# Row sums of the modulation, one per step and tied to VectorE's latest scan operation, in a GLA and SSD backbone

## The chip, the cores and the metric

The kernel runs on one NeuronCore of a Trainium2 chip. The metric is the device time of one execution in microseconds (us). The engines are TensorE (PE, matmuls), VectorE (DVE), ScalarE (ACT), GpSimd (POOL) and SyncE (SP, which issues the DMAs). Each engine works its instructions off in the order in which the program lists them, and waits for the others through semaphores.

## What is computed

A two-layer backbone over 512 latent and 256 context tokens of width 1024. Layer 0 mixes tokens by bidirectional gated linear attention (GLA, 4 heads), layer 1 by a Mamba-2 scan (SSD); each is followed by a squared-ReLU MLP, and each sub-layer is modulated by six vectors, for latent and context tokens apart.

```python
for i in range(DEPTH):
    ...
    m_l = jnp.split((s_lat @ ada_w[i] + ada_b[i])[:, None, :], 6, axis=-1)
    m_c = jnp.split(s_ctx @ ada_w[i] + ada_b[i], 6, axis=-1)
    ul = snake(modulate(hl, m_l[0], m_l[1]))
    uc = modulate(hc, m_c[0], m_c[1])
    ...
    hl = layer_norm(DEEPNORM_ALPHA * hl + m_l[2] * snake(yl), ln_g[i, 0], ln_b[i, 0])
    hl = layer_norm(DEEPNORM_ALPHA * hl + m_l[5] * sq_relu_mlp(modulate(hl, m_l[3], m_l[4]), ffn_w1[i], ffn_w2[i]),
                    ln_g[i, 1], ln_b[i, 1])
    ...
```

Here DEPTH is 2, `hl` and `hc` are the latent and the context tokens, and `yc, yl` come from the mixer of the layer, given `uc, ul`.

Inside one head of the GLA mixer, with q, k of width 128 and v of width 256:

```python
cum = jnp.cumsum(gi, axis=2)
diff = cum[:, :, :, None, :] - cum[:, :, None, :, :]
decay = jnp.exp(jnp.where(mask, diff, -jnp.inf))
attn = jnp.einsum('bhid,bhjd,bhijd->bhij', qi, ki, decay)
o = jnp.einsum('bhij,bhjv->bhiv', attn, vi) + jnp.einsum('bhid,bhdv->bhiv', qi * jnp.exp(cum), s)
```

`gi` is the log decay of a chunk and `s` the state that the chunks before it left.

## The kernel before

Activations lie transposed, features on the 128 partitions and the 768 tokens along the free axis. A product of float32 accuracy is made of three matmuls over split operands: ScalarE rounds a weight tile to its high half (`wh`, L218), VectorE subtracts to get the low half (`wl`, L219), and PE runs high by high, low by high and high by low (L265; L547 for the values). `worked(cols)` counts the columns of these matmuls; every 768 make one unit, and the units are the clock by which other work is woven in while the program is written out.

Two lists hang on that clock. `side` holds generators that say after each step how many units to wait for the next. `background` holds the row sums: one step every `pace[0]` units.

**Row sums.** `ada_rows` computes those modulation vectors that aren't made by matmuls. For each item (layer, m) and block b of 128 rows it loads a 128x1024 weight block (`rawa`, SP, three buffers, which the thrown-away output `junk` shares in the GLA layer) and runs one scalar_tensor_tensor with a row sum (L172) for each of the two streams; for layer 1's later vectors only the latent stream is needed. A step covers one block, so two row sums for most blocks. `behind()` lists a row sum directly behind the instruction held in `evacv`, if one is held. Before the change `evacv` is set only in the two functions that take FFN and output products out of PSUM, so in the whole GLA scan part it is empty, and the scheduler of the program places the row sums freely.

**GLA.** `head(h)` makes q, k, v and two gate projections for one head on PE. The scan of the head before it, `scan(h-1)`, runs as a `side` generator at the same time, so scans 1 to 3 lie beside the projections of heads 1 to 3 and scan 4 beside the output projection. A scan starts from the log decays W (L590), and then goes through seven levels, s = 1, 2, ..., 64. In a level ScalarE takes exponentials of W into E (L629, L630), VectorE multiplies them by q and k (L631), GpSimd and VectorE update W (L639 to L642), PE makes the score blocks from E (L601), and VectorE copies the scores of the level before into A under a mask (L620; L617 for s = 64). Then W becomes the decayed q and k (the decay products, L653 and L654, in two halves), PE transposes them (L664), makes the state updates (L672), VectorE chains the states (L683, L685), PE makes outputs (L703), which are normalized (L705 to L708), transposed (L730) and gated (L731). This last part, from the decay products on, is called the tail.

**FFN.** `ffn` runs its two products in blocks of eight row tiles, with its own paces for the row sums of layer 1, which run beside it.

Of the kernel before, what the change touches and what calls it, by code (L numbers as in the profile page):

```python
# [13 lines left out]
ALU = mybir.AluOpType  # L14
PSUM = bass.MemoryType.PSUM

P = 128
# [43 lines left out]
def tile_backbone(ctx, tc, xT, cc, cr, vecs, rows, ada_w0, ada_wr, lnf, ffn_w1, ffn_w2,  # L61
# [52 lines left out]
    evacv = [None]  # L114

    def behind():
        return tc.issue_after(evacv[0].ins) if evacv[0] else nullcontext()
# [30 lines left out]
    def ada_rows(items, alloc, junk):  # L148
        srow = [alloc(s) for s in range(2)]
        for s in range(2):  # L150
            nc.sync.dma_start(srow[s], cr[s:s + 1, :].to_broadcast([P, D]))
            nc.scalar.activation(srow[s], srow[s], AF.Silu)
        def load(layer, m, b):
            raw = wpool.tile([P, D], F32, tag="rawa", name=nm("rawa"), bufs=3)
            nc.sync.dma_start(raw, ada_wr[48 * layer + 8 * m - 16 + b])
            return raw

        todo = [(layer, m, b) for layer, m in items for b in range(8)]
        raws = [load(*todo.pop(0))]
        yield  # L160
        for layer, m in items:
            streams = range(1 if layer and m > 1 else 2)
            t = ct([P, 8, 2], f"row{layer}{m}")
            nc.gpsimd.memset(t, 0.0)
            for b in range(8):
                if todo:
                    raws.append(load(*todo.pop(0)))
                raw = raws.pop(0)
                for s in streams:
                    o = raw if s == streams[-1] else junk()  # L170
                    with behind():
                        nc.vector.scalar_tensor_tensor(o, raw, 1.0, srow[s], ALU.mult, ALU.mult, accum_out=t[:, b, s:s + 1])  # L172
                yield
            c0 = V_ADA + 48 * layer + 8 * m
            nc.vector.tensor_tensor(t, t, vec[:, c0:c0 + 8].unsqueeze(2).to_broadcast([P, 8, 2]), ALU.add)
            mods[layer, m] = t
# [211 lines left out]
    def ffn(layer, xs, acc, segs, pool, npre, presegs, restsegs, passes, after):  # L388
# [27 lines left out]
        for bi, nb in enumerate((8, 8, 8, 8 - nlast, nlast)):  # L416
            ms = range(h0, h0 + nb)
            if bi == 0:
# [6 lines left out]
                for m in ms[:npre]:  # L425
                    f1(m, restsegs, held[m])
                pace[0] = 19
                ms = ms[npre:]
# [6 lines left out]
            if bi == 0:  # L435
                gate = mod(layer, 5)
                pace[0] = 22
            if bi < 4:
# [48 lines left out]
    def gla_layer(xs, first):  # L487
# [20 lines left out]
        background.append(ada_rows([(0, 2), (0, 3), (0, 4)], lambda s: xn_tile(f"srow{s}"), lambda: wpool.tile([P, D], F32, tag="rawa", name=nm("junk"), bufs=3)))  # L508
        pace[0] = 12
        aT = gp.tile([P, NT], F32R, tag="aT", name="aT")  # L510
# [41 lines left out]
        def head(h):  # L552
# [19 lines left out]
            if h == 0:  # L572
                pace[0] = 22
            side.append(scan(h, qk, v, gs, yt))

        def scan(h, qk, v, gs, yt):
# [38 lines left out]
            def level(s, E):  # L615
                if s == HP:
                    scores(E[:, 1, :], E[:, 0, :], lambda b, a, sp, bs, qs: (nc.scalar.copy, nc.vector.tensor_copy)[b](a, sp), 1)  # L617
                else:
                    scores(qk[:, 1, :] if s == 1 else E[:, 1, :], E[:, 0, :],
                           lambda b, a, sp, bs, qs: nc.vector.copy_predicated(  # L620
                               a, lvm[s][bs, qs].unsqueeze(1).to_broadcast(half), sp))

            for s in (1, 2, 4, 8, 16, 32, 64):
# [6 lines left out]
                nc.scalar.activation(Ev[:, 0:na, :, 0, :], Wv[:, 2:2 + na, :, 0, :], AF.Exp, scale=1.0 / 16)  # L630
                nc.vector.tensor_mul(E[:, 0:na, :], E[:, 0:na, :], qk[:, 0:na, :])  # L631
                bc = [P, nb, s]
# [8 lines left out]
                nc.vector.tensor_add(Wv[:, 0, :, 1, :], Wv[:, 0, :, 1, :], Wv[:, 0, :, 0, s - 1:s].to_broadcast(bc))  # L641
                nc.vector.tensor_add(Wv[:, 2, :, 0, :], Wv[:, 2, :, 0, :], Wv[:, 2, :, 1, 0:1].to_broadcast(bc))  # L642
                yield LV[h][0]
# [8 lines left out]
            for a, b in ((1, 1), (0, 0)):  # L652
                nc.scalar.activation(W[:, a:4:2, :], W[:, a:4:2, :], AF.Exp, scale=1.0 / 16)  # L653
                nc.vector.tensor_mul(W[:, a:4:2, :], W[:, a:4:2, :], qk[:, b:b + 1, :].to_broadcast([P, 2, NT]))  # L654
            yield 1
# [24 lines left out]
            def step(S, i, a, d):  # L680
                t = new_S()
                if S is None:
                    nc.vector.tensor_copy(t, d[:, 1 - a, :])  # L683
                else:
                    nc.vector.scalar_tensor_tensor(t, S, dec[:, a, i:i + 1], d[:, 1 - a, :], ALU.mult, ALU.add)  # L685
                return t
# [8 lines left out]
            def output(c):  # L695
# [9 lines left out]
                nc.scalar.activation(on[:, c, :], op, AF.Square, accum_out=rs)  # L705
                nc.vector.tensor_scalar(rs, rs, 1.0 / 256, RMS_EPS, ALU.mult, ALU.add)
                nc.gpsimd.tensor_tensor(rs, rs, mhalf[:, 0:1], ALU.pow)
# [17 lines left out]
            for c2 in range(2):  # L725
                for c0, c1 in SEG:
                    pt = sm_ps([P, 4, P])
                    ts = slice(c0 * P, c1 * P)
                    for c in range(c0, c1):
                        nc.tensor.transpose(pt[:, c - c0, :], on[:, c, c2 * P:(c2 + 1) * P], ident)  # L730
                    nc.vector.scalar_tensor_tensor(yt[c2][:, ts], pt.rearrange("p c t -> p (c t)")[:, :(c1 - c0) * P],  # L731
                                                   vec[:, V_GN + c2:V_GN + c2 + 1], gs[c2][:, ts], ALU.mult, ALU.mult)
# [519 lines left out]
    with phase("fp") as fp:  # L1252
        pace[0] = 21
        background.append(ada_rows([(0, 5)] + [(1, m) for m in range(6)],
# [93 lines left out]
```

## Time and profile before

| what | value |
| --- | --- |
| median of 3 runs | 1938.48 us (1937.09 to 1941.59) |
| profiled execution, its own time | 1938.47 us |
| its span | 1936.8 us |
| instructions in the span | 28836 |
| row sums (L172), 128x1024, those that write over their input, x80 | 99.7 us, mean 1252 ns |
| weight split, low half (L219) x225 | 271.1 us, mean 1208 ns |
| score matmuls and projections of scans 1 to 3 | about 95 to 310 us of the span |
| first FFN, PE without a gap | 447 to 957 us |

The page of a profile gives busy time by engine, the chain of work that ended last (followed back from the last instruction to what released each step), and groups of instructions by line. In a timeline row stand the start, the duration in us, the engine, the line, the operation with output and inputs, the count, and in brackets the idle time ahead of it with what ended it. In a row of stretches stand the stretch, its length, the busy time of the engines or of the chosen instructions, TensorE's granted clock as a share of full speed, the DMA share and GB/s.

### The profile page before, as it was taken

Reading aid. Unit: us, or ns where it says so; the run is one execution under the profiler, and the core shown is the slowest. Engines: PE = TensorE matmul, PEld = TensorE weight load, DVE = VectorE, ACT = ScalarE, POOL = GpSimd, SP = SyncE. Lnnn points to the kernel's source line nnn. Section 1 sums busy time; section 2 is a strip of 40 time slices with the busy share of each in tenths; the row PEclk is TensorE's granted clock in tenths of the full one; section 3 lists DMA queues with packets and bytes.
Section 4 is the critical chain, followed back from the end, with each engine's and each line's share of the span. In section 5 each row is a group of like instructions: output and inputs, shape, how many; then the busy total and the mean of one; then the engine's idle time right before and its main releaser. Section 6 shows DMA issues by size and latency. Waiting matters only on the chain.

```text
span 1936.8 us, 28836 instructions
## 1 busy us (share of the span) xinstructions
PE 1877.8 (97%) x11365; PEld 1602.2 (83%) x11365; DVE 1265.8 (65%) x1932; ACT 795.8 (41%) x1387; POOL 392.4 (20%) x363
## 2 busy tenths in 40 slices
PE   7989999999999999999998999999999999999997
PEld 5978898788888888888897778888877788888886
DVE  4998877977655434433477989999896673333345
ACT  4445456456213113112274555556564452323231
POOL 2033241302102002000001333323331321102012
PEclk9999999999999999999999999999999999999999
DMA  9624203122444444323225333343443523333331
GB/s 354 192 73 134 77 26 98 38 91 89 151 134 123 135 129 133 120 93 98 66 68 136 120 115 121 113 126 127 131 125 115 170 71 97 98 98 98 95 90 54
DMA packets 78999, 219.07 MB, mean 113 GB/s; under 512 B 11088, under 2 KB 15824, under 8 KB 78864
## 3 DMA queue, kind: packets, MB, share of 16 engines
q1 hardware_dynamic: 78864, 217.24, 35.7%
q8 instruction: 89, 1.46, 0.3%
q14 instruction: 46, 0.38, 0.1%
HBM read 209.07 MB, written 8.13 MB: 112 GB/s over the span
## 4 chain that ended last, share of the span: by engine, by line
PE 60%; DVE 17%; issue 9%; ACT 6%; POOL 4%; DMA 4%; SPq 1%; DVEq 0%; ACTq 0%; POOLq 0%
PE mm L265 53%; DVE cv L911 4%; DMA L<-crowc 2%; DVE cf L914 2%; DVE wl L219 1%; DVE A L620 1%; PE sm L703 1%; POOL L L1048 1%; POOL W L639 1%; PE mm L547 1%; DVE E L631 1%; DMA raw<-in_ada_w_dram 1%; POOL ssum L1089 1%; DVE lnst L330 1%; ACT xn L340 1%
## 5 line engine op out<-in xcount | busy, mean ns | idle before, releaser
L265 PE MATMUL mm<-xh,wh 128*128 128x512 f32 (+1 forms) x1800 | 551.3, 360 | 2.2 <-ACT xh L1096 2.2
L265 PE MATMUL mm<-xl,wh 128*128 128x512 f32 (+1 forms) x1800 | 545.3, 356 | 3.8 <-DVE xl L1097 3.8
L265 PE MATMUL mm<-xh,wl 128*128 128x512 f32 (+1 forms) x1800 | 543.5, 355 | 0.8 <-DVE wl L219 0.8
L218 ACT CAST wh<-raw 128x1024 fp32r<-128x1024 f32 (+3 forms) x225 | 226.1, 1006 | 656.9 <-PE mm L265 621.1
L219 DVE TENSOR_TENSOR wl<-raw,wh 128x1024 fp32r<-128x1024 f32 (+3 forms) x225 | 271.1, 1208 | 199.5 <-ACT wh L218 195.7
L265 PEld LDWEIGHTS mm<-xl,wh 128*128 128x128 f32 x1800 | 300.8, 189 | 55.4 <-DVE xl L1097 5.0
L265 PEld LDWEIGHTS mm<-xh,wh 128*128 128x128 f32 x1800 | 300.1, 189 | 53.8 <-issue 4.7
L265 PEld LDWEIGHTS mm<-xh,wl 128*128 128x128 f32 x1800 | 298.8, 189 | 50.1 <-issue 2.0
L410 POOL TENSOR_TENSOR rq<-rr 128x768 f32<-128x768 f32 (+1 forms) x62 | 102.4, 1652 | 735.5 <-ACT rr L409 732.7
L446 DVE SCALAR_TENSOR_TENSOR acc<-mm,row,acc 128x256 f32<-128x256 f32 (+1 forms) x182 | 100.6, 580 | 212.6 <-PE mm L265 212.2
L265 PE MATMUL mm<-rh,wh 128*128 128x512 f32 x704 | 215.1, 359 | 0.0
L265 PE MATMUL mm<-rl,wh 128*128 128x512 f32 x704 | 212.5, 355 | 0.0
L265 PE MATMUL mm<-rh,wl 128*128 128x512 f32 x704 | 212.4, 355 | 0.0
L911 DVE SCALAR_TENSOR_TENSOR cv<-pre,cvec,cv 128x770 f32<-128x770 f32 (+1 forms) x128 | 149.7, 1170 | 12.6 <-ACT cv L909 10.8
L265 PEld LDWEIGHTS mm<-rl,wh 128*128 128x128 f32 x704 | 117.0, 189 | 21.4
L265 PEld LDWEIGHTS mm<-rh,wl 128*128 128x128 f32 x704 | 115.3, 188 | 20.3
L265 PEld LDWEIGHTS mm<-rh,wh 128*128 128x128 f32 x704 | 116.1, 188 | 19.2
L412 DVE TENSOR_TENSOR rl<-rq,rh 128x768 fp32r<-128x768 f32 (+2 forms) x67 | 53.3, 795 | 76.2 <-POOL rq L410 75.9
L172 DVE SCALAR_TENSOR_TENSOR rawa<-rawa,srow 128x1024 f32<-128x1024 f32 x80 | 99.7, 1252 | 0.8
L1045 ACT ACTIVATE L<-L,lcol 128x128 f32<-128x128 f32 x256 | 80.1, 393 | 0.0
L1048 POOL TENSOR_TENSOR L<-L,L 128x512 f32<-128x512 f32 x32 | 49.0, 1530 | 151.1 <-ACT L L1045 151.1
L958 POOL TENSOR_SCALAR_AFFINE_SELECT L<-L 128x512 f32<-128x512 f32 x64 | 53.6, 838 | 119.5 <-DMA L<-crowc 111.1
(295 smaller groups left out, 2514.2 us busy)
## 6 DMA issues: line engine op xcount, KB each, us to landing
raw<-in_ffn_w_dram SPq DMA_DIRECT2D x112, 512.0 KB, 3.8
rawa<-in_ada_wr_dram SPq DMA_DIRECT2D x80, 512.0 KB, 3.6
raw<-in_ssd_w_in_dram SPq DMA_DIRECT2D x48, 512.0 KB, 3.6
L<-crowc SPq DMA_DIRECT2D x64, 256.0 KB, 3.8
raw<-in_ada_w_dram SPq DMA_DIRECT2D x16, 512.0 KB, 9.2
raw<-in_gla_w_in_dram SPq DMA_DIRECT2D x16, 512.0 KB, 4.5
ec<-crow SPq DMA_DIRECT2D x64, 128.0 KB, 2.9
acc<-in_xT_dram SPq DMA_DIRECT2D x14, 384.0 KB, 6.9
```

Source lines behind the costliest of these rows:

```text
L172: nc.vector.scalar_tensor_tensor(o, raw, 1.0, srow[s], ALU.mult, ALU.mult, accum_out=t[:, b, s:s + 1])
L218: nc.scalar.copy(h, src)
L219: nc.vector.tensor_sub(l, src, h.bitcast(F32))
L265: nc.tensor.matmul(part_of(ps, t0, n), a[:, k, :], b[:, t0:t0 + n], start=(k == 0 and i == 0), stop=(k == kt - 1 and i == 2))
L410: eng.tensor_mul(q[:, a:b], r[:, a:b], r[:, a:b])
L412: evacv[0] = nc.vector.tensor_sub(rl[:, a:b], q[:, a:b], rh[:, a:b].bitcast(F32))
L446: evacv[0] = nc.vector.scalar_tensor_tensor(acc[m][:, t0:t0 + n], part_of(ps, t0, n), gate[:, m, s:s + 1], (src or acc)[m][:, t0:t0 + n], ...
L911: nc.vector.scalar_tensor_tensor(c[:, 0:n], pre[:, t:t + n], cw(t), c[:, 0:n], ALU.mult, ALU.add)
L914: nc.vector.scalar_tensor_tensor(f[:, t0:t1], f[:, t0:t1], 1.0, c[:, t0 + d:t1 + d], ALU.add, ALU.mult)
L958: nc.gpsimd.affine_select(out=L[z], in_=L[z], compare_op=ALU.is_ge, fill=NEG, base=0, pattern=[[0, 4], [1 - 2 * z, P]], channel_multiplier ...
L1045: nc.scalar.activation(t[:, h, :], t[:, h, :], AF.Exp, bias=lcol[:, c, r:r + 1])
L1048: nc.gpsimd.tensor_add(L[0], L[0], L[1])
```

## The change

Four things change. `ada_rows` gives out one row sum per step, not a block's pair. The paces are about halved (12 to 6 and 22 to 11 in the GLA layer, 19 to 10, 22 to 12 and 21 to 11 around the first FFN), so that about as many row sums come per unit where blocks have two, and twice as many where blocks have one. A helper `mark` puts an instruction into `evacv`, and seven places in the scan use it: the masked score copies, the multiply of E, the second update of W, the decay products, the state steps, the variance of the outputs and the gated outputs. So from the first scan on a row sum is listed behind the latest of these.

```diff
+    def mark(ins):
+        evacv[0] = ins
+
@@ ada_rows
                     with behind():
                         nc.vector.scalar_tensor_tensor(o, raw, 1.0, srow[s], ALU.mult, ALU.mult, accum_out=t[:, b, s:s + 1])
-                yield
+                    yield
@@ ffn, gla_layer, head and the LayerNorm ahead of the first FFN
-                pace[0] = 19
+                pace[0] = 10
...
-                pace[0] = 22
+                pace[0] = 12
...
-        pace[0] = 12
+        pace[0] = 6
...
-                pace[0] = 22
+                pace[0] = 11
...
-        pace[0] = 21
+        pace[0] = 11
@@ scan: level
-                           lambda b, a, sp, bs, qs: nc.vector.copy_predicated(
-                               a, lvm[s][bs, qs].unsqueeze(1).to_broadcast(half), sp))
+                           lambda b, a, sp, bs, qs: mark(nc.vector.copy_predicated(
+                               a, lvm[s][bs, qs].unsqueeze(1).to_broadcast(half), sp)))
@@ scan: the seven levels
-                nc.vector.tensor_mul(E[:, 0:na, :], E[:, 0:na, :], qk[:, 0:na, :])
+                mark(nc.vector.tensor_mul(E[:, 0:na, :], E[:, 0:na, :], qk[:, 0:na, :]))
...
-                nc.vector.tensor_add(Wv[:, 2, :, 0, :], Wv[:, 2, :, 0, :], Wv[:, 2, :, 1, 0:1].to_broadcast(bc))
+                mark(nc.vector.tensor_add(Wv[:, 2, :, 0, :], Wv[:, 2, :, 0, :], Wv[:, 2, :, 1, 0:1].to_broadcast(bc)))
@@ scan: decay products, state steps, outputs
-                nc.vector.tensor_mul(W[:, a:4:2, :], W[:, a:4:2, :], qk[:, b:b + 1, :].to_broadcast([P, 2, NT]))
+                mark(nc.vector.tensor_mul(W[:, a:4:2, :], W[:, a:4:2, :], qk[:, b:b + 1, :].to_broadcast([P, 2, NT])))
...
-                    nc.vector.scalar_tensor_tensor(t, S, dec[:, a, i:i + 1], d[:, 1 - a, :], ALU.mult, ALU.add)
+                    mark(nc.vector.scalar_tensor_tensor(t, S, dec[:, a, i:i + 1], d[:, 1 - a, :], ALU.mult, ALU.add))
...
-                nc.vector.tensor_scalar(rs, rs, 1.0 / 256, RMS_EPS, ALU.mult, ALU.add)
+                mark(nc.vector.tensor_scalar(rs, rs, 1.0 / 256, RMS_EPS, ALU.mult, ALU.add))
...
-                    nc.vector.scalar_tensor_tensor(yt[c2][:, ts], pt.rearrange("p c t -> p (c t)")[:, :(c1 - c0) * P],
+                    evacv[0] = nc.vector.scalar_tensor_tensor(yt[c2][:, ts], pt.rearrange("p c t -> p (c t)")[:, :(c1 - c0) * P],
```

The changed file has three more lines ahead of `ada_rows`, so each line number there is three higher (L172 becomes L175, L219 L222, L620 L623, L631 L634, L641 and L642 L644 and L645, L654 L657).

How the order changes is read from the listed order of each engine. First VectorE at the end of scan 1's levels, s = 32 and 64, where `lvm` is a level's mask, `sm` a score block in PSUM and `raw`, `wh`, `wl` a weight tile and its halves. Before:

```order
L620 COPY_PREDICATED A_958<-lvm_618,sm_1327 64x6x64 x2
L172 SCALAR_TENSOR_TENSOR rawa_1583,row_1311<-rawa_1583,srow_91_703 128x1024
L631 TENSOR_TENSOR E_1363<-E_1363,qk_644 128x1536
L641 TENSOR_TENSOR W_924<-W_924 128x6x64
L642 TENSOR_TENSOR W_924<-W_924 128x6x64
L620 COPY_PREDICATED A_958<-lvm_624,sm_1383 64x6x64 x2
L654 TENSOR_TENSOR W_924<-W_924,qk_644 128x2x768 x2
```

And of the change:

```order
L175 SCALAR_TENSOR_TENSOR junk_1320,row_1195<-rawa_1197,srow_90_684 128x1024
L623 COPY_PREDICATED A_963<-lvm_618,sm_1331 64x6x64 x2
L634 TENSOR_TENSOR E_1367<-E_1367,qk_644 128x1536
L644 TENSOR_TENSOR W_928<-W_928 128x6x64
L645 TENSOR_TENSOR W_928<-W_928 128x6x64
L175 SCALAR_TENSOR_TENSOR rawa_1197,row_1195<-rawa_1197,srow_91_685 128x1024
L623 COPY_PREDICATED A_963<-lvm_624,sm_1388 64x6x64 x2
L222 TENSOR_TENSOR wl_1410<-raw_1407,wh_1409 128x1024
L657 TENSOR_TENSOR W_928<-W_928,qk_644 128x2x768 x2
```

The row sum stands ahead of the score copy instead of behind it, another one and the split of a weight tile stand ahead of the decay products. Before, that tile's split stands 15 rows above L654, in the fourth level.

PE reads this split. At the same place of scan 1, before:

```order
L601 MATMUL sm_1383<-E_1299 64x64 x12
L265 MATMUL mm_1400<-xh_105,wh_1404 128x512
L265 MATMUL mm_1401<-xh_105,wh_1404 128x256
L265 MATMUL mm_1400<-xl_106,wh_1404 128x512
L265 MATMUL mm_1401<-xl_106,wh_1404 128x256
L265 MATMUL mm_1400<-xh_105,wl_1405 128x512
```

And of the change:

```order
L268 MATMUL mm_1546<-xh_105,wh_1549 128x256
L268 MATMUL mm_1545<-xl_106,wh_1549 128x512
L604 MATMUL sm_1436<-E_1367 64x64 x12
L268 MATMUL mm_1546<-xl_106,wh_1549 128x256
L268 MATMUL mm_1405<-xh_105,wl_1410 128x512
L268 MATMUL mm_1406<-xh_105,wl_1410 128x256
```

Before, the low half is first read 5 rows behind the scores of s = 32. Now four matmuls of the next tile are drawn ahead of it, and the scores of s = 64 as well, directly ahead of its first use; the first transposes of W follow 24 rows, or 12 units, behind that use.

VectorE again, in scan 3 at s = 32, before:

```order
L631 TENSOR_TENSOR E_2821<-E_2821,qk_1675 128x1536
L641 TENSOR_TENSOR W_2461<-W_2461 128x12x32
L642 TENSOR_TENSOR W_2461<-W_2461 128x12x32
L620 COPY_PREDICATED A_2495<-lvm_618,sm_2848 64x6x64 x2
L631 TENSOR_TENSOR E_2881<-E_2881,qk_1675 128x1536
L641 TENSOR_TENSOR W_2461<-W_2461 128x6x64
L642 TENSOR_TENSOR W_2461<-W_2461 128x6x64
L654 TENSOR_TENSOR W_2461<-W_2461,qk_1675 128x2x768
L620 COPY_PREDICATED A_2495<-lvm_624,sm_2901 64x6x64 x2
L654 TENSOR_TENSOR W_2461<-W_2461,qk_1675 128x2x768
```

And of the change:

```order
L634 TENSOR_TENSOR E_2826<-E_2826,qk_1680 128x1536
L644 TENSOR_TENSOR W_2465<-W_2465 128x12x32
L645 TENSOR_TENSOR W_2465<-W_2465 128x12x32
L175 SCALAR_TENSOR_TENSOR junk_2842,row_2130<-rawa_2721,srow_90_684 128x1024
L623 COPY_PREDICATED A_2500<-lvm_618,sm_2852 64x6x64 x2
L634 TENSOR_TENSOR E_2885<-E_2885,qk_1680 128x1536
L644 TENSOR_TENSOR W_2465<-W_2465 128x6x64
L645 TENSOR_TENSOR W_2465<-W_2465 128x6x64
L175 SCALAR_TENSOR_TENSOR rawa_2721,row_2130<-rawa_2721,srow_91_685 128x1024
L623 COPY_PREDICATED A_2500<-lvm_624,sm_2906 64x6x64 x2
L222 TENSOR_TENSOR wl_2940<-raw_2937,wh_2939 128x1024
L657 TENSOR_TENSOR W_2465<-W_2465,qk_1680 128x2x768 x2
```

Scan 3's levels held no row sum; now six of the seven hold one, the last score copy stands ahead of both decay products, and a split stands between it and them. In scan 2's stretch, from L590 to the split behind the decay products, there are nine row sums where there were six. POOL's order is the same in both, and so are the scans of layer 1 and the second FFN.

## Prediction, made before the changed kernel was run

> **What bounds the kernel now.** I read the busy times first, then the chain that ended last, then busy time by stretches of the span, then the row sums alone in the same stretches, and last the timelines of the three attention scans.
>
> ```profile
> PE 1877.8 (97%) x11365; PEld 1602.2 (83%) x11365; DVE 1265.8 (65%) x1932; ACT 795.8 (41%) x1387; POOL 392.4 (20%) x363
> PE 60%; DVE 17%; issue 9%; ACT 6%; POOL 4%; DMA 4%; SPq 1%; DVEq 0%; ACTq 0%; POOLq 0%
> 447.00:957.00 510.00, 510.00 (x2914) 443.31 (x2913) 242.49 (x352) 123.48 (x178) 53.85 (x31) 1.00 0.38 120
> ```
>
> TensorE (PE) is busy 97% of the span and holds 60% of the chain that ended last; VectorE (DVE) comes second there with 17%. PE runs without a gap from 447 to 957 us (columns: stretch, its length, then PE, weight loads, VectorE, ScalarE, GpSimd). That is the first FFN. Whatever the change does there to DVE lies beside a full PE, so I cost the new FFN paces at nothing; PE itself is the cover, and without it a row sum costs its own 1.25 us (the first row below). What is open is the GLA layer ahead of it, where PE and DVE take turns in three scans.
>
> ```profile
> L172 DVE SCALAR_TENSOR_TENSOR rawa<-rawa,srow 128x1024 f32<-128x1024 f32 x80 | 99.7, 1252 | 0.8
> 95.00:140.00 45.00, 5.08 (x8) 1.00 0.16 48
> 140.00:170.00 30.00, 18.44 (x30) 0.94 0.62 193
> 170.00:224.00 54.00, 10.61 (x16) 0.97 0.23 69
> 260.00:304.00 44.00, 0.00 (x0) 1.00 0.16 50
> ```
>
> The four lower rows are the row sums alone (each counted twice, with its accumulator read): scan 1's levels hold 4 (one of them ahead of the first multiply), its tail 15, scan 2's stretch 8 (6 of them behind L590), scan 3 none. By the order of the changed kernel, 7 stand between scan 1's first decay multiply (L631, s=1) and its first decay product (L654), 4 in its tail, 9 between scan 2's L590 and the weight split behind its products, 6 in scan 3's levels. Scan 4 holds none in either. I take 1.27 us for each: the mean with its 0.02 us between neighbours. All of them run in both kernels; what changes is which work stands behind each one. DVE takes its instructions strictly as they stand, so a sum that is put behind a level's update of W holds up the score copy and the next multiply that stand after it, and through them ScalarE's exponentials and PE's scores.
>
> A row sum also frees the buffer into which SP loads the next rows, and SP's weight loads stand in the same queue:
>
> ```profile
> raw<-in_gla_w_in_dram SPq DMA_DIRECT2D x16, 512.0 KB, 4.5
> ```
>
> If a weight load came late for that reason it would cost up to these 4.5 us. I cost it at nothing: four raw weight buffers are filled ahead, and the sums that come later in scans 2 and 3 come one by one, so SP waits oftener but for less. The high end below has room for one such load.
>
> **Why a row sum in a level costs.** One level is a ring: DVE multiplies E (L631) and updates W (L641, L642), ScalarE takes the next exponentials, GpSimd adds (L639), DVE copies scores (L620), multiplies again.
>
> ```profile
> 204.81 2.43 DVE L631 TENSOR_TENSOR E<-E,qk 128x1536 f32<-128x1536 f32 x1
> 209.48 1.93 DVE L172 SCALAR_TENSOR_TENSOR rawa<-rawa,srow 128x1024 f32<-128x1024 f32 x1
> 211.34 1.75 DVE L631 TENSOR_TENSOR E<-E,qk 128x1536 f32<-128x1536 f32 x1
> 213.95 1.21 DVE L172 SCALAR_TENSOR_TENSOR junk<-rawa,srow 128x1024 f32<-128x1024 f32 x1
> 216.47 1.82 DVE L631 TENSOR_TENSOR E<-E,qk 128x1536 f32<-128x1536 f32 x1
> ...
> 285.11 1.76 DVE L631 TENSOR_TENSOR E<-E,qk 128x1536 f32<-128x1536 f32 x1
> 287.61 0.56 DVE L641 TENSOR_TENSOR W<-W 128x384 f32<-128x384 f32 x1 [0.74 <-POOL W L639]
> 289.92 1.76 DVE L631 TENSOR_TENSOR E<-E,qk 128x1536 f32<-128x1536 f32 x1
> ```
>
> From multiply to multiply a level without a row sum takes 289.92-285.11 = 4.81 us, 0.74 of it DVE waiting for GpSimd. With the sum behind the copies it takes 211.34-204.81 = 6.53, with the sum ahead of them 216.47-211.34 = 5.13. Most of the new sums stand ahead, so the dearer order is partly mended: the price of a new sum lies between 0.3 us (wait swallowed) and 1.7 us. PE's own work per level decides whether it shows:
>
> ```profile
> 185.69 0.92 PE L601 MATMUL sm<-E,qk 128*64 128x64 f32 x24
> 191.02 0.92 PE L601 MATMUL sm<-E 128*64 128x64 f32 x24
> 134.37 0.53 PE L265 MATMUL mm<-xh,wh 128*128 128x512 f32 x2
> 134.73 0.51 PE L265 MATMUL mm<-xl,wh 128*128 128x512 f32 x2
> ```
>
> In scan 2, PE's pace is 5.33 us a level; and a unit of 768 columns (one 512 and one 256 matmul) takes 0.36.
>
> **Scan 1.**
>
> ```profile
> 116.75 1.23 DVE L219 TENSOR_TENSOR wl<-raw,wh 128x1024 fp32r<-128x1024 f32 x1
> ...
> 134.18 3.43 DVE L654 TENSOR_TENSOR W<-W,qk 128x1536 f32<-128x1536 f32 x2
> ...
> 136.09 0.63 PE L664 MATMUL sm<-ident,W 128*128 128x128 f32 x4 [0.84 <-DVE W L654]
> ...
> 145.50 0.70 PE L703 MATMUL sm<-v,A 128*128 128x256 f32 x2 [1.67 <-DVE W L685]
> ...
> 164.99 2.16 PE L730 MATMUL sm<-ident,on 128*128 128x128 f32 x9 [1.95 <-ACT on L708]
> ```
>
> Added ahead of L654: 4 row sums (5.1 us) and one more split (two where one stood, 1.2). Taken back: about 0.8, since ScalarE's first exponentials now stand ahead of a weight cast, and 2.2 of the dearer order and of waits for GpSimd. That leaves +3.3 (2.2 to 4.7), so L654 starts near 137.5. The split that ran at 116.75, in the fourth level, now stands behind the last sum and the last score copy and ends just there. PE needs its result 12 units ahead of the first transposes, so they come at 137.5+12x0.36 = 141.8, and L654 itself, which they waited for before, is done by then. Against 136.09, and with 2 units (0.7) of projection done early, PE is 5.0 late (3.9 to 6.4, as more or fewer of the waits go). In the tail 4 sums stand where 15 did, so I let both waits go, 1.67+1.95 = 3.6. The granted clock (column behind PE's busy time) adds to that:
>
> ```profile
> 165.00:169.00 4.00, 4.00 (x17) 0.57 0.64 203
> 219.00:223.00 4.00, 4.00 (x25) 0.58 0.00 0
> ...
> 132.01 0.92 PE L601 MATMUL sm<-E 128*64 128x64 f32 x24 [1.79 <-DVE E L631]
> ...
> 218.43 0.92 PE L601 MATMUL sm<-E 128*64 128x64 f32 x24 [1.74 <-DVE E L631]
> ```
>
> The waits of 1.95 and 1.74 us are each followed by 4 us at 0.57 and 0.58, that is 4x0.42 = 1.7 us lost; those of 1.79 (at 132) and 1.67 are not. So the tail returns 3.6+1.6 = 5.2. Scan 1: 5.0-5.2 = **-0.2**, bounds -1.3 and +1.2, or up to +6.4 if the tail's waits stay.
>
> The Trainium skill, "TensorE: Matmul & The Clock Gate", section "HAM oscillation — how this bites in real kernels", sums its rule up as "no PE-idle gaps >~3.4µs". This trace disagrees: half that wait sufficed twice. By the rule the tail's 1.6 would not come back and the total below would be 1.6 higher; the measurement decides.
>
> **Scan 2.**
>
> ```profile
> DVE E L631 <- ACT E L630: 1.2, 2, 1.0
> DVE W L641 <- POOL W L639: 1.1, 1, 1.1
> ...
> 224.50 2.36 DVE L219 TENSOR_TENSOR wl<-raw,wh 128x1024 fp32r<-128x1024 f32 x2
> ```
>
> PE's next stop behind the levels is the first of the two splits at 224.50, done at 225.7. Three more row sums stand ahead of it, 3.8 us. DVE's waits in those levels are 2.3 (two upper rows: sum, count, longest); swallowed, they leave 1.5. But one split and one sum (1.2 and 1.3) that stood ahead of the first multiply, where DVE waited for ScalarE anyway, now stand behind it too: 3.8+2.5 = 6.3. I take 1.5 of the 2.3 as swallowed, because the waits before the first multiply remain: **+4.8**, bounds 1.5 and 6.3. Behind this split I give nothing back.
>
> **Scan 3.**
>
> ```profile
> DVE W L641 <- POOL W L639: 3.5, 4, 1.1
> DVE W L641 <- ACT E L629: 1.1, 1, 1.1
> DVE E L631 <- ACT E L630: 1.0, 1, 1.0
> DVE W L654 <- ACT W L653: 0.5, 1, 0.5
> ...
> 293.93 1.76 DVE L654 TENSOR_TENSOR W<-W,qk 128x1536 f32<-128x1536 f32 x1 [0.49 <-ACT W L653]
> ...
> 295.83 0.63 PE L664 MATMUL sm<-ident,W 128*128 128x128 f32 x4 [0.87 <-DVE W L654]
> ...
> 300.61 1.97 PE L672 MATMUL sm<-v,kn 128*128 128x256 f32 x8 [0.83 <-DVE A L617]
> ```
>
> PE already waits for L654 (0.87), so delay shows at once. Six sums (7.6) and a score copy moved ahead of L654 (1.2) make 8.8. Waits of 6.1 (first four rows) could swallow all but 2.7. I take ScalarE's last two (1.5) whole and half of GpSimd's 3.5, since a sum directly ahead of a multiply holds GpSimd's addition up, or is held up by it, as at 209.48: 3.25. That gives 5.5 at the transposes, and the 0.83 behind them goes: **+4.7**, bounds 1.9 and 8.8. The split of this scan moves from the middle of the levels to their end, which leaves DVE's total as it is, but PE now needs it 7 units ahead of the transposes (2.5 us), about when L654's first half is done, so neither adds to the other.
>
> **Sum.** -0.2+4.8+4.7 = 9.3. PE's new waits ahead of scan 1's and scan 2's late splits come to about 3 us each, longer than the two that cost clock. Part of such a spell lies beside a later wait; I charge one, 1.65 (bounds 0 and three, 5). So +10.95 on the profiled execution's 1938.47 (span 1936.8), which is the median's 1938.48: **1949.4 us**. All low bounds together, -1.3+1.5+1.9 = 2.1, give 1940.6; all high ones, 1.2+6.3+8.8+5 = 21.3, give 1959.8, but not together.
>
> **Rivals.** *Faster:* a sum ahead of the copies makes a level of 5.13 us, under PE's 5.33 in scan 2. If that holds in all three scans, no multiply is late where PE reads it, and only the tail's relief stays: 1938.5-5.2 = 1933.3. It decides as soon as levels stay under PE's pace. Against it: in scan 3 PE is already the one that waits, and splits (1.2) join sums in the same level. 12%. *No change:* waits swallow all they can, 1940.6; 17%. *Tail not relieved:* its two waits hang on the exponentials' engine rather than on the sums; then scan 1 gives +5.0 and the total is 5.0+4.8+4.7+1.65 = 16.2, or 1954.6; inside the slower part, 10%. *The change doing nothing:* excluded, the order of DVE's rows differs in all three scans.
>
> **How the numbers follow.** The forecast has 61% and slower in all 71%. A measurement of this kernel tells about 0.2% (3.9 us) from no change, so faster is under 1934.6, slower over 1942.4: 12, 17 and 71%. The range of 8 in 10 reaches from 1937.5, which leaves out the faster rival, to 1956.0, past the unrelieved tail.
>
> **What would show it.** Right: PE waits of about 3 us for a split's low half (wl) ahead of the first transposes of scan 1, and again in scan 2; L654's first row 3, 5 and 5 us later behind each scan's first multiply; no wait for W of L685 or the `on` rows in scan 1's tail; the first FFN at 510 us as before. Wrong: score matmuls that never wait, or a wait of PE inside the FFN, which would mean that the new pace touches the loads there; or half-clock spells after short waits, which would add 1.65 each.

## The result, and the profile after

The change is slower, by 0.8%: 1954.12 us median (1953.55 to 1957.29, 4 runs) against 1939.51 (1937.09 to 1941.59, 4 runs), a ratio of 1.0079 with a 95% interval of 1.0064 to 1.0093. The profiled execution's span is 1951.8 us where it was 1936.8, 15.0 more.

First the page of the changed kernel: busy time by engine, and the chain that ended last.

```profile
PE 1881.9 (96%) x11365; PEld 1604.6 (82%) x11365; DVE 1267.7 (65%) x1932; ACT 796.0 (41%) x1387; POOL 392.1 (20%) x363
PE 61%; DVE 16%; issue 9%; ACT 6%; POOL 4%; DMA 3%; SPq 0%; DVEq 0%; ACTq 0%; POOLq 0%
```

No engine has more work than before: DVE's busy time grew by 2 us, PE's by 4 (the clock, below). The page can't say where 15 us went. Positions of the same work in both traces can. Here are the first score matmuls (diagonal blocks, `sm<-qk`) of scans 2, 3 and 4 in PE's timeline, before:

```profile
171.93 0.92 PE L601 MATMUL sm<-qk 128*64 128x64 f32 x24
...
252.09 0.92 PE L601 MATMUL sm<-qk 128*64 128x64 f32 x24
...
329.56 0.92 PE L601 MATMUL sm<-qk 128*64 128x64 f32 x24
```

and in the changed kernel:

```profile
173.70 0.92 PE L604 MATMUL sm<-qk 128*64 128x64 f32 x24
...
259.39 0.92 PE L604 MATMUL sm<-qk 128*64 128x64 f32 x24
...
343.26 0.92 PE L604 MATMUL sm<-qk 128*64 128x64 f32 x24
```

The delay is 1.8, 7.3 and 13.7 us at these three points, and 14.0 at the first ReLU of the FFN (443.7 before, 457.7 now). So 14 of 15 us are lost in scans 1 to 3, and scan 4, which has no row sums, only passes them on. Scan 1 began 0.6 us earlier, so the three scans themselves take 2.3, 5.5 and 6.4 us more.

What PE waits for in the GLA layer, by group (us in total, times, longest), in the changed kernel:

```profile
PE sm L604 <- DVE E L634: 11.4, 11, 2.3
PE mm L268 <- DVE wl L222: 8.4, 4, 3.3
PE mm L550 <- DVE wl L222: 2.0, 2, 1.2
...
PE sm L667 <- DVE W L657: 0.9, 1, 0.9
```

Waits for the levels' multiply grew from 7.0 to 11.4 us, and waits for weight splits from 0.8 to 10.4. Of the three waits for the decay product ahead of a transposition that of scan 4 is left; in scans 1 and 3 a wait for a split stands in their place. PE's timeline shows the places:

```profile
136.88 1.01 PE L268 MATMUL mm<-xh,wl 128*128 128x512 f32 x2 [3.33 <-DVE wl L222]
...
143.48 0.60 PE L667 MATMUL sm<-ident,W 128*128 128x128 f32 x4
...
167.50 1.47 PE L733 MATMUL sm<-ident,on 128*128 128x128 f32 x12
...
214.79 0.92 PE L604 MATMUL sm<-E 128*64 128x64 f32 x24 [2.31 <-DVE E L634]
...
220.11 1.01 PE L268 MATMUL mm<-xh,wl 128*128 128x512 f32 x2 [1.47 <-DVE wl L222]
...
307.66 0.62 PE L268 MATMUL mm<-xh,wl 128*128 128x512 f32 x2 [2.75 <-DVE wl L222]
```

And DVE's timeline, the end of scan 1's levels, shows why that split is late:

```profile
132.65 0.55 DVE L645 TENSOR_TENSOR W<-W 128x384 f32<-128x384 f32 x1
133.12 1.21 DVE L175 SCALAR_TENSOR_TENSOR rawa<-rawa,srow 128x1024 f32<-128x1024 f32 x1
...
134.37 1.20 DVE L623 COPY_PREDICATED A<-lvm,sm 64x384 f32<-64x384 uint8 x2
135.60 1.23 DVE L222 TENSOR_TENSOR wl<-raw,wh 128x1024 fp32r<-128x1024 f32 x1
136.75 3.42 DVE L657 TENSOR_TENSOR W<-W,qk 128x1536 f32<-128x1536 f32 x2
```

DVE has no gap here. It ends the split at 136.8, PE starts at 136.9. The scan-1 tail's two long waits (for W of L685 and for `on`) are gone, as forecast: the row at 167.50, which had one of them, shows no wait. The granted clock (column behind PE's busy time) in the three stretches of scans 1 to 3 in which it was halved:

```profile
135.09:141.92 6.83, 5.04 (x15) 0.50 0.26 77
217.01:223.84 6.83, 4.95 (x14) 0.50 0.49 155
309.17:312.58 3.41, 3.41 (x14) 0.50 0.39 126
```

Half clock stands at all three late splits, but it doesn't always begin behind them. In scan 1 it sets in at 135.1, while PE waits. In scan 2 it sets in at 217.0, behind the wait for E (to 214.8) and within one of 1.28 us for `v`, ahead of the wait for the split.

Added up as (1 - clock) x length, half clock comes to 8.5 us in scans 1 to 3, against 3.4 before (3.41 us each at 165 and at 220); scan 4 has 1.7 in both. PE was busy in only 13.4 of these 17.1 us, so an estimate of what half clock cost its work is half of that, 6.7 us, which is 3.3 more than before.

### The profile page after: what moved, and what is told of

The parts are those of the page before. It is cut to its first block, busy times and chain, and to the rows that moved or that the text cites. A ratio compares the mean times of both kernels' runs of the same rounds, so it can differ in the third digit from the quotient of the medians.

```text
span 1951.8 us, 28828 instructions
## 1 busy us (share of the span) xinstructions
PE 1881.9 (96%) x11365; PEld 1604.6 (82%) x11365; DVE 1267.7 (65%) x1932; ACT 796.0 (41%) x1387; POOL 392.1 (20%) x363
## 4 chain that ended last, share of the span: by engine, by line
PE 61%; DVE 16%; issue 9%; ACT 6%; POOL 4%; DMA 3%; SPq 0%; DVEq 0%; ACTq 0%; POOLq 0%
PE mm L268 53%; DVE cv L914 4%; DMA L<-crowc 2%; DVE cf L917 2%; DVE A L623 1%; PE sm L706 1%; POOL L L1051 1%; DVE wl L222 1%; PE sm L675 1%; PE mm L1199 1%; PE mm L550 1%; DVE E L634 1%; POOL ssum L1092 1%; DVE lnst L333 1%; DVE W L644 1%
## 5 line engine op out<-in xcount | busy, mean ns | idle before, releaser
L222 DVE TENSOR_TENSOR wl<-raw,wh 128x1024 fp32r<-128x1024 f32 (+3 forms) x225 | 271.2, 1209 | 197.3 <-ACT wh L221 193.6
L268 PEld LDWEIGHTS mm<-rl,wh 128*128 128x128 f32 x704 | 117.0, 189 | 21.5
L175 DVE SCALAR_TENSOR_TENSOR rawa<-rawa,srow 128x1024 f32<-128x1024 f32 x80 | 98.1, 1241 | 0.3
```

Of the source, the lines that this page charges most:

```text
L222: nc.vector.tensor_sub(l, src, h.bitcast(F32))
L268: nc.tensor.matmul(part_of(ps, t0, n), a[:, k, :], b[:, t0:t0 + n], start=(k == 0 and i == 0), stop=(k == kt - 1 and i == 2))
```

## Experiments

All kernels are compared with runs of the kernel before on the same chip (medians of 1938.3 to 1939.5 us). The table gives their median time, the ratio with its 95% interval, and, from one profiled execution each, the length of the four scans (from one scan's first score matmul to the next one's; scan 4 to the FFN's first ReLU) and from there to the end of the span, all in us.

| kernel | time | ratio | scan 1 | scan 2 | scan 3 | scan 4 | FFN to end |
| --- | --- | --- | --- | --- | --- | --- | --- |
| before | 1939.5 | 1 | 84.1 | 80.2 | 77.5 | 114.1 | 1493.1 |
| the change | 1954.1 | 1.0079 (1.0064 to 1.0093) | 86.4 | 85.7 | 83.9 | 114.4 | 1494.1 |
| change_again | 1954.4 | 1.0085 (1.0072 to 1.0098) | 86.5 | 85.8 | 83.9 | 114.3 | 1494.0 |
| no_marks | 1935.9 | 0.9989 (0.9980 to 0.9999) | 83.5 | 77.2 | 76.7 | 113.1 | 1496.3 |
| marks_only | 1945.3 | 1.0033 (1.0019 to 1.0046) | 79.9 | 84.6 | 80.8 | 114.4 | 1497.4 |
| old_ffn_pace | 1950.4 | 1.0060 (1.0045 to 1.0075) | 86.1 | 85.6 | 83.8 | 114.3 | 1490.9 |
| no_level_sums | 1942.3 | 1.0014 (1.0005 to 1.0024) | 77.2 | 83.6 | 82.4 | 114.2 | 1496.4 |
| free_scan3 | 1954.3 | 1.0078 (1.0065 to 1.0090) | 87.9 | 86.0 | 79.2 | 117.0 | 1494.8 |
| splits_ahead | 1947.2 | 1.0039 (1.0026 to 1.0051) | 81.9 | 83.5 | 81.2 | 113.1 | 1497.0 |
| before_splits_ahead | 1944.7 | 1.0030 (1.0020 to 1.0040) | 85.0 | 81.0 | 79.5 | 113.1 | 1495.9 |
| filled_waits | 1958.5 | 1.0098 (1.0084 to 1.0111) | 85.3 | 86.5 | 85.2 | 114.2 | 1498.0 |
| tail_marks | 1942.8 | 1.0023 (1.0014 to 1.0031) | 76.7 | 83.9 | 85.0 | 114.4 | 1494.9 |
| no_marks_old_ffn | 1938.4 | 0.9999 (0.9987 to 1.0011) | 83.5 | 77.2 | 76.7 | 113.1 | 1493.7 |

The last column differs by some us between kernels whose program is the same from the first FFN on. The trace shows half-clock spells in layer 1 at the same places of the program, more of them in some executions than in others. So the scans' columns carry the argument, and whole times within 3 us of each other aren't told apart by it. The scans' columns have a spread too: scan 1 of the change, of change_again, old_ffn_pace and free_scan3 is the same program, and took 86.1 to 87.9 us.

### Which half of the change costs

The change without the marks (single steps and new paces stay):

```diff
     def mark(ins):
-        evacv[0] = ins
+        pass
...
-                    evacv[0] = nc.vector.scalar_tensor_tensor(yt[c2][:, ts], pt.rearrange("p c t -> p (c t)")[:, :(c1 - c0) * P],
+                    nc.vector.scalar_tensor_tensor(yt[c2][:, ts], pt.rearrange("p c t -> p (c t)")[:, :(c1 - c0) * P],
```

> The change with its paces and single steps, but no mark in the scans, so the row sums there are placed freely again. VectorE's order in scans 1 to 3 then is nearly that of before (3 row sums in scan 1's levels, none in scan 3's). Theory (row sums inside the levels lengthen VectorE's ring and delay a weight split): 1936 to 1942 us, like before. Rival (the single steps and halved paces are the cause, through the loads they trigger or the number of interruptions): 1950 us or more. FFN pieces are the same in both.

And the marks without the rest:

```diff
                         nc.vector.scalar_tensor_tensor(o, raw, 1.0, srow[s], ALU.mult, ALU.mult, accum_out=t[:, b, s:s + 1])
-                    yield
+                yield
...
-        pace[0] = 6
+        pace[0] = 12
...
-                pace[0] = 11
+                pace[0] = 22
```

(and the paces 19, 22 and 21 of before at the FFN)

> Before with only the marks: row sums in pairs at the old paces, each pair tied to the latest scan operation. VectorE's levels then hold row sums in all three scans (6, 7 and 6), often two in one level. Theory (sums in levels): 1946 to 1956 us, with a wait of PE for E or for a split of 2 us or more in each of the three scans. Rival (pace): 1938 to 1942 us.

Without marks the time is 1935.9, a shade faster than before, so single steps and halved paces cost nothing by themselves. Its trace shows full clock through all scans, which is a part of scan 2's 3 us under before (1.7 at most). The marks alone cost 6.6 us (1945.3 against 1938.65), a little less than expected. The wait of 2 us or more came in scans 1 (2.23 us) and 2, but not in scan 3, where the longest is 1.61. Both together cost 15: with pairs the scheduler left scan 1's split two levels further up, PE waits there for E and not for a split, and the scan is even 4.2 us shorter than before, since the tail is relieved too. The rival falls and "sums in the levels" holds, but much seems to hang on where the splits end up, which is tried below.

PE's wait in scan 2 of marks_only, which is its largest:

```profile
218.03 1.55 PE L604 MATMUL sm<-E 128*64 128x64 f32 x24 [4.47 <-DVE E L634]
```

### Taking the sums out of levels

The change with the row sums held back in the levels, and pace 5:

```diff
-            if clock[1] % pace[0] == 0:
+            if clock[1] % pace[0] == 0 and not hold[0]:
                 advance(background)
...
             late = []
+            hold[0] = 1
...
             level(*late.pop())
+            hold[0] = 0
...
-                pace[0] = 11
+                pace[0] = 5
```

> The change, but no row sum is given out between the first scores of a scan and its last score copy, and pace 5 in place of 11 in the GLA layer, so the row sums fall into the tails of the scans and ahead of the levels, still tied by marks. Theory (sums in levels are the cost): the 14 to 15 us go, 1934 to 1941 us; below 1938 if the tails stay free of waits of over 1 us. Rival (pace or ties as such): 1948 us or more.

Scan 1 takes 77.2 us, 9.2 less than with the change and 6.9 less than before. But the sums come back behind the levels. DVE's timeline of that kernel at the end of scan 2:

```profile
213.65 1.76 DVE L658 TENSOR_TENSOR W<-W,qk 128x1536 f32<-128x1536 f32 x1
215.33 1.22 DVE L175 SCALAR_TENSOR_TENSOR rawa<-rawa,srow 128x1024 f32<-128x1024 f32 x1
...
217.18 1.23 DVE L175 SCALAR_TENSOR_TENSOR junk<-rawa,srow 128x1024 f32<-128x1024 f32 x1
...
218.33 3.49 DVE L222 TENSOR_TENSOR wl<-raw,wh 128x1024 fp32r<-128x1024 f32 x3
```

Two sums stand between the decay products and the split that PE needs next, and PE waits 3.96 us for it, with half clock behind. Scans 2 and 3 are 3.4 and 4.9 us longer than before. The time, 1942.3, is 1.3 over the expected range: here row sums cost outside the levels too, where DVE is what PE waits for next.

The same for scan 3 alone (`hold[0] = h == 2`, paces as with the change):

> The change, but scan 3 alone gets no row sum between its first scores and its last score copy; the six sums come later, in its tail and in scan 4. Theory (each scan pays for the sums in its own levels): scan 3 costs 6.4 us with the change (by the first score matmuls of scans 3 and 4, 7.3 and 13.7 us late); those go, less 1 to 3 us that the displaced sums cost behind: 1948 to 1951 us, scan 1 and 2 as with the change. Rival (the delay is handed on from scan to scan, so that scan 3 only passes on what scans 1 and 2 lost): 1953 us or more.

The time, 1954.3, is the rival's, but the scans are not: scan 3 takes 4.7 us less than with the change, so it didn't merely pass on earlier delay. Nothing is won, because scan 4, which now gets three of the displaced sums, takes 2.6 more, and scan 1, whose program is the change's, took about 1.4 more, with half clock at 110 that the change didn't have there. So my 1 to 3 us for the displaced sums held in scan 4; the forecast missed because scan 3 gave back 4.7 and not 6.4, and by scan 1's clock. In PE's timeline of that kernel, scan 4 has new waits:

```profile
354.34 0.50 PE L268 MATMUL mm<-xh,wh 128*128 128x512 f32 x1 [1.68 <-DVE acc L449]
356.31 1.55 PE L604 MATMUL sm<-E 128*64 128x64 f32 x24 [1.24 <-DVE E L635]
358.80 0.58 PE L268 MATMUL mm<-xh,wh 128*128 128x256 f32 x1 [0.93 <-DVE acc L449]
```

The change without the three marks inside the levels (score copies, E, W), with those on the decay products and in the tail:

```diff
-                           lambda b, a, sp, bs, qs: mark(nc.vector.copy_predicated(
-                               a, lvm[s][bs, qs].unsqueeze(1).to_broadcast(half), sp)))
+                           lambda b, a, sp, bs, qs: nc.vector.copy_predicated(
+                               a, lvm[s][bs, qs].unsqueeze(1).to_broadcast(half), sp))
...
```

> The change with its paces and single steps, but without the three marks inside the levels (score copies, multiply of E, update of W); those on the decay products and in the tail stay. VectorE's order then has no row sum in scan 1's levels, five in scan 2's, and scan 3's are as with the change, split ahead of the decay products included. Theory (each scan pays for the sums in its own levels): scan 1 takes 5 to 7 us less than before (as without sums in levels), scan 2 up to 4 more than before, scan 3 5 to 7 more, together 1940 to 1945 us. Rival (single sums between level operations cost time wherever the program puts them, through their number): 1950 us or more.

The time, 1942.8, is as expected, and so are the scans within half a us: no sum in scan 1's levels, and the scan takes 76.7 us, 7.4 under before; scan 3, whose levels are as with the change, takes 7.5 more than before. Scan 2 is 3.7 over, though by its trace its levels hold six sums where before has five. PE waits there 3.93 us for a split that stands behind them. So the cost goes scan by scan with the scan's own levels, but not by the number of sums alone.

### The late split

The change with gate tiles and first tiles loaded and split one projection earlier:

```diff
-        def transposed(m, evac):
+        ahead = {}
+
+        def transposed(m, evac, nxt=None):
...
-                prod(ps, weights(gla_w_in, m), xs, BOTH, KT)
+                w = ahead.pop(m, None) or weights(gla_w_in, m)
+                if nxt is not None:
+                    ahead[nxt] = weights(gla_w_in, nxt)
+                prod(ps, w, xs, BOTH, KT)
...
+            m = 8 + 2 * h + (h == 0)
+            ahead[m] = weights(gla_w_in, m)
...
-                transposed(8 + 2 * h + c2, lambda ts, ps: nc.scalar.activation(gt[:, ts], ps, AF.Silu))
+                nxt = 9 + 2 * h if c2 == 0 else h + 1 if h < GH - 1 else None
+                transposed(8 + 2 * h + c2, lambda ts, ps: nc.scalar.activation(gt[:, ts], ps, AF.Silu), nxt if h or c2 else None)
```

> The change, but each gate tile's weights are loaded and split one projection earlier (and so is each head's first tile), so that the split of which PE waits stands two to four levels earlier on VectorE; as many row sums in the levels as with the change. Theory (the sums push the last split behind the levels and PE waits 3.3, 1.5 and 2.8 us for it, with half clock behind): PE then waits for the decay products instead, which end 4 to 5 us before the transposes in scan 1 and about 2 in scans 2 and 3: 1945 to 1949 us. Rival (the ring alone sets the time, the split only shows it): 1952 us or more.

The same edit on the kernel before:

> Before, with the same earlier loads and splits and nothing else. Theory (before has no late split ahead of a transposition): little to gain, 1935 to 1942 us. Rival (earlier splits help any order): as much as splits_ahead gains against the change, 1930 us or less.

PE's waits in the GLA layer of splits_ahead:

```profile
PE sm L612 <- DVE E L642: 11.6, 11, 3.5
...
PE mm L557 <- DVE wl L222: 1.3, 2, 0.7
PE sm L675 <- DVE W L665: 1.2, 2, 0.9
...
PE mm L268 <- DVE wl L222: 0.8, 1, 0.8
```

The waits for splits fell from 10.4 to 2.1 us, those for E stayed at 11.6, and the kernel takes 1947.2, in the expected range, 7 us less than the change. The scans are 4.5, 2.2 and 2.7 us shorter than with the change; half clock in them comes to 6.8 us against 8.5, so most of this is not the clock. On the kernel before the same edit costs 6 us: I expected no effect, and the rival a gain, so both missed. Its scans are 0.9, 0.8 and 2.0 us longer and scan 1 starts 1.5 us later (the first tile's split comes in its way). So the gain isn't that earlier splits are good; it is that the change had made some of them late.

### The clock

Ten unused matmuls behind the scores of s = 64 in scans 1 and 3 of the change:

```diff
                 if s == HP:
                     scores(E[:, 1, :], E[:, 0, :], lambda b, a, sp, bs, qs: (nc.scalar.copy, nc.vector.tensor_copy)[b](a, sp), 1)
+                    if h in (0, 2):
+                        fl = sm_ps([P, 256])
+                        for _ in range(10):
+                            nc.tensor.matmul(fl, E[:, 1, 0:P], E[:, 0, 0:256], start=True, stop=True)
```

> The change, with ten extra matmuls (128x256, 0.22 us each, result unused) behind the scores of s = 64 in scans 1 and 3, eight of which stand where PE waits 3.3 and 2.8 us for the split. They fill about 1.7 us of each wait and give PE about 0.4 us more work behind. Theory (a wait of over about 1.7 us is followed by about 3.4 us or more at half clock): both spells go, 1949 to 1952 us. Rival (the spells have another cause, or the wait left over is enough): 1954 to 1956 us with both spells in the trace.

Each took 0.43 us and not 0.22, so eight of them filled the wait whole. Neither range came: the kernel takes 1958.5. PE's granted clock in five stretches of that kernel:

```profile
108.00:112.00 4.00, 2.83 (x30) 0.63 0.11 46
137.00:141.00 4.00, 4.00 (x21) 1.00 0.38 135
216.00:220.00 4.00, 1.90 (x5) 0.50 0.13 22
302.00:306.00 4.00, 2.48 (x27) 0.70 0.01 2
309.00:313.00 4.00, 4.00 (x24) 1.00 0.46 131
```

Where the waits were filled, at 137 and 309, the clock stays at 1.00. But half clock now stands at two other waits, at 109 and 303. The one at 109 lies ahead of the first extra matmul. In PE's timeline its wait is:

```profile
109.17 1.55 PE L604 MATMUL sm<-E 128*64 128x64 f32 x24 [2.11 <-DVE E L638]
```

The same wait of 2.11 us in the change is followed by full clock:

```profile
108.36 0.92 PE L604 MATMUL sm<-E 128*64 128x64 f32 x24 [2.11 <-DVE E L634]
```

The kernel as a whole is slower than the change: half clock comes to 8.5 us up to 440 us as with the change, scan 1 is 1.1 us shorter, scans 2 and 3 are 0.8 and 1.3 longer, and 3.9 us come behind the FFN, where the program is the same. So a wait is needed for a spell, and filling it keeps the clock, but the length of the wait alone doesn't decide.

The changed kernel once more:

> The changed kernel itself once more, for what varies between executions of one program. The starts of scans 2, 3 and 4 should lie within 2 us of the first profile's (173.7, 259.4, 343.3), 1952 to 1956 us; if half-clock spells fall by a free-running window and not by the length of a wait alone, some of them stand at other places than 134, 216 and 308 us. If the length of the wait decides alone, all three are there again.

```profile
137.00:141.00 4.00, 3.84 (x12) 0.50 0.40 131
219.00:223.00 4.00, 2.55 (x8) 0.50 0.67 168
309.00:313.00 4.00, 4.00 (x18) 0.57 0.48 130
```

The starts of the scans agree within 0.5 us, and the three spells stand at the same places.

What decides between two programs with the same wait at nearly the same time can be read from the traces. In each of the 13, all changes of the granted clock from 15 us to the end lie whole multiples of 3.41 us apart. How this grid lies against the scans can differ from execution to execution. Here are two neighbouring stretches of the grid around the wait that ends at 108.36 us in the change, with PE's busy time and the clock:

```profile
104.37:107.79 3.42, 1.88 (x32) 1.00 0.50 151
107.79:111.20 3.41, 2.18 (x33) 1.00 0.01 2
```

And around the same wait, of 2.10 us up to 108.44, in free_scan3, whose program is the same up to there:

```profile
106.29:109.70 3.41, 1.31 (x28) 1.00 0.35 126
109.70:113.11 3.41, 2.80 (x14) 0.50 0.13 24
```

In the change a boundary of the grid divides the wait, PE is idle for 1.54 us of the first stretch, and the clock stays full. In free_scan3 the whole wait falls into one stretch, PE is idle for 2.10 us of it, and the next stretch runs at half clock. The other stretches agree. From 60 us on, the 13 traces have 69 stretches at full clock in which PE was idle for 1.9 us or more, and all were followed by half clock; they have 6923 with less than 1.6 us, and none was; of 33 in between, 16 were. So it isn't the length of a wait that decides here, but how much of PE's idle time falls into one stretch of the grid, with the limit near half of it.

In the two executions of the change the grid lies alike (half clock first sets in 38.6 us ahead of scan 2's scores in both). So the repeated places don't show that the spells belong to the program; with the grid elsewhere a spell can come or go, as in scan 1 of free_scan3.

### The paces in the FFN

The change with the old FFN paces, and no_marks with them:

```diff
-                pace[0] = 10
+                pace[0] = 19
...
-                pace[0] = 12
+                pace[0] = 22
...
-        pace[0] = 11
+        pace[0] = 21
```

> The change, but with the old paces 21, 19 and 22 ahead of and in the first FFN (single steps stay, so half as many row sums per unit there). Theory (PE covers the FFN's row sums): 1952 to 1956 us, as with the change, FFN stretch as long as before. Rival (faster row sums in the FFN cost time): 1948 us or less.

> No mark in the scans, as in no_marks, and in and ahead of the first FFN the old paces 21, 19 and 22. With the marks the old paces took 3.6 us less, nearly all of it between the start of the first FFN and the convolutions of layer 1, where PE's pairs of matmuls came every 0.345 us instead of 0.352. If that goes with the paces, it comes again: 1931 to 1934 us. If it was a matter of that program's alignment: 1935 to 1939 us.

The scans are as with the change, but the FFN isn't: from its first ReLU to layer 1's first convolution it is 577.9 us, against 580.8 with the change and before. Neither number that I expected came. A stretch in the middle, PE busy throughout, of old_ffn_pace:

```profile
600.00:700.00 100.00, 100.00 (x579) 1.00 0.32 99
```

and of the change:

```profile
600.00:700.00 100.00, 100.00 (x569) 1.00 0.50 158
```

The count in brackets is higher by 1.8% at the same clock. In the timeline of the same stretch a pair of matmuls comes every 0.347 us instead of 0.353 on average (one pair of three takes 0.361 in the change), from a single wait onward:

```profile
537.50 0.50 PE L268 MATMUL mm<-rh,wh 128*128 128x512 f32 x1 [0.91 <-DVE acc L449]
```

In no_marks_old_ffn the faster pairs are there again (579 in the same stretch), behind a wait of 0.96 us at 519.15, but the times spread from 1934.0 to 1943.1 with a median of 1938.4. So the profiled execution, 1934.05, lies at the edge of the first branch of the expectation, the median in the second, and this kernel isn't shown to be better than no_marks. Why the pace changes at that wait stays open. No version beats both kernels by much; no_marks does by 0.1%, at the edge of its interval.

## Why the prediction was right, and where its size was off

**FFN at nothing: right for the change.** It takes 580.8 us to layer 1's first convolution in both. Single sums at the old paces made it 2.9 shorter, by a cause the prediction didn't know.

**Late loads at nothing: right too.** No engine waits for a weight load in scans 1 to 3 of the change.

**Scan 1: right in its steps.** I put the start of L654 at 137.5; it came at 136.75. I put the split's end there and PE's wait for it at about 3 us; it was 3.33. The tail's waits of 1.67 and 1.95 went. What was off is behind the wait: 12 units, most of them at half clock, took 6.6 us (136.88 to 143.48), not 4.3, so the transposes came at 143.5 and not 141.8. The scan cost 2.3 where I had -0.2.

**Scan 2: the size about right, the place wrong.** Forecast +4.8, measured +5.5. I had put PE's wait, of about 3 us, at the split behind the decay products. It came in front of them: 2.31 us for E, then 1.28 for `v` and 1.47 for a split in the last level. Half clock set in during the second of these, and half clock behind short waits is one of the signs that I had named for being wrong.

**Scan 3: low, and the split not free.** Forecast +4.7, measured +6.4, with a spell of 1.7 us at 309 in it that I hadn't charged here. I had the transposes wait for L654, with the split done in time. PE waited for the split instead, 2.75 us, and the 7 units behind it brought the transposes to 311.1, 8.0 us later in the scan than before and not 5.5.

**The mis-sized term: half clock.** I returned 1.6 us in scan 1's tail and charged one spell of 1.65, a net of about nothing. The change has half clock at three places of its scans, 17.1 us long in all, where before has two of 3.41. By the estimate above, which counts only the time in which PE was busy, that is 3.3 us net. The three scans lost 14.2 us, against 9.3 + 1.65 = 10.95 in my sum, so half clock accounts for about the 3.2 us between them; the rest of 1954.1 - 1949.4 lies outside these scans and in the spread of the runs. Without clock losses the scans lost 14.2 - 3.3 = 10.9 us, as in my 9.3 + 1.6 with the tail's clock not returned. That this comes out so well is partly luck, since in scans 2 and 3 the wait that counted stood elsewhere than I had it. It is partly luck, too, that the range held the time: its upper end, 1956.0, was drawn past the rival of the unrelieved tail, which did not happen.

**The rivals.** *Faster* failed on its condition and as its counter-argument said. In scan 1 levels with a sum ahead of the copies took 5.2 us (L634 at 119.97, 125.23 and 130.45), not over PE's 5.33, but the last level's sum, copy and split ended late all the same. In scan 2 most sums stand behind the copies, and its levels took 5.8, 5.8 and 7.6 us (L634 at 200.72, 206.54, 212.34 and 219.98), the last with a split in it. *Tail not relieved* gave nearly the right time, 1954.6, for the wrong reason: the tail was relieved, as 167.50 without a wait shows. *No change* failed because only part of DVE's waits swallowed sums.

**The rule on the clock.** The Trainium skill, "TensorE: Matmul & The Clock Gate", section "HAM oscillation — how this bites in real kernels", asks for no PE gap over about 3.4 us. This case disagrees: half clock came with waits of 2.75 and 3.33 us, and with one of 2.11 in one program and not in another, where the grid divided it. The measurements decide: shorter waits can cost clock on this chip.

## What to carry to other kernels

Work that is off the path can still set the time by its place in an engine's queue: ask not only whether the engine has room, but which later instruction stands behind it and who waits for that one. Tying helper work to the latest step of a dependent ring puts it into the ring; left free, it fell into gaps that the scheduler had. When an edit moves such work, look for the nearest operand of the busiest engine (here a weight split) that slides behind it, and allow for half clock behind a wait of about 2 us or more, for it can cost nearly as much as the wait (2.3 us behind 3.33 in scan 1).

## What the runs showed of the hardware that was not expected

PE's pace in a long run of matmuls has two values at the same granted clock: pairs of a 512 and a 256 column matmul every 0.353 us on average, or, after a wait of 0.91 us at 537.5 (0.96 at 519.2 in the other program), every 0.347, to the end of that FFN (569 against 579 matmul records in 100 us). It came in both programs with the old FFN paces and single steps; in all others the stretch from the FFN's first ReLU to layer 1's first convolution took 580.8 us. And the granted clock changes on a grid of 3.41 us: a stretch in which PE was idle for 1.9 us or more was followed by half clock in all 69 cases, one with less than 1.6 in none of 6923, so that the same wait can cost a spell in one execution and nothing in another.
